# Mixers and experts on one core: first chunk as whole float32, POOL's work elsewhere, router sums moved

## The chip, the core and the metric

The kernel runs on one core of one Trainium2 chip. The metric is device time in microseconds (us). Before the change the median of three runs is 862.81 us (861.21 to 863.67). The engines are PE (TensorE, matrix products), ACT (ScalarE), DVE (VectorE), POOL (GpSimd) and SP, which here only sends for data. Each works its own instructions in order.

## The reference

Two layers, 256 tokens, 1024 channels, everything in float32. A layer is a mixing sublayer and a mixture of experts, each followed by a layer norm over the sum with the residual:

```python
z = h @ w_in[l]                       # ten blocks of 256 columns, and four gates of 1024
branches = (short_conv, rg_lru, gmlp, retention)      # 256 columns each
merged = sum(sigmoid(gate[b]) * (branches[b] @ branch_proj[l, b]) for b in range(4))
h = layer_norm(ALPHA * h + merged @ w_out[l])
# router: one of 4 groups, then 2 of its 8 experts for each token
out = sum(combine[:, e] * ((silu(h @ w_gate[e]) * (h @ w_up[e])) @ w_down[e]) for e in range(32))
h = layer_norm(ALPHA * h + out)
```

## The kernel before

**Weights.** They come in chunks of 1 MB, in the order in which they are used: 34 of a mixing sublayer, then 96 of the experts, then the next layer. `Ring` holds 22 slots of 1 MB; `pump` (line 99) sends for the next chunk on SP's queue whenever a slot beyond the reserve for larger buffers is free, and a few loads of parameters are hung before certain chunks (`before`, line 176): `params` of layer 1 (line 259), with the pack `rp` that holds the router's weights, goes out before the fifth chunk of layer 1.

**The mixing sublayer** (`mixer`, line 350). Every chunk is four pieces of 512 columns. For accuracy a piece is split in two (`do_split`, line 337; `hilo`, line 254): ACT casts it to float32r, which gives the leading bits (`whi`), and DVE subtracts that from the piece (`wlo`). The rows of the layer's input are split in the same way (`hThi`, `hTlo`). A product is then three products (`tripled`, line 323):

```python
nc.tensor.matmul(out, ah, bh, start=first and i == 0, stop=False, skip_group_check=True)
nc.tensor.matmul(out, ah, bl, start=False, stop=False, skip_group_check=True)
nc.tensor.matmul(out, al, bh, start=False, stop=stop_last and i == n - 1, skip_group_check=True)
```

Splits run four pieces (LOOK) ahead of their products. The order of everything else is set by generators: after the products of each piece `advance` (line 463) runs each generator to its next `yield`, so a `yield` is one piece of the sublayer's products. The four branches are such generators: `g_ret` (555), `g_lru` (639), `g_sgu` (683), `g_sc` (721). Some of their elementwise steps are POOL's: the sum of the two rope parts (573), the products of lines 663 and 673, the subtraction of the means in `std64` where it works in place (537), the products 620, 621, 697 and 714, and the Newton steps of the root (`rsqrt`, 305). The retention branch ends in transposes on PE (628), which need line 621.

With the first gate two more things start: `residual` (917), POOL's, which multiplies the rows by ALPHA (layer 0: one instruction of 128x2048; layer 1: also gain and bias of the norm before, from a slot `gb` that SP loads), and `g_router` (280), which sums the router's weights with the norm's gain and bias on PE, DVE and POOL.

**Norm and router** (`norm_mix`, line 780). The rows are summed, their statistics taken, the router's products made from the transposed sums (`rt`, one bank for both halves of the tokens; DVE copies one half, ACT the other), and the logits `lg` formed by four small DVE instructions after the product `raw`.

**The experts** (`moe`, line 1029). For each of eight groups of four experts the tokens are gathered by a product with a one-hot matrix (`gather`, 1142), multiplied with eight chunks (line 1052), and with four more on the way back (1102, 1089). Every chunk gives its slot back when its product is written.

**From layer 0 to layer 1** (`norm_ffn`, line 864). The sums are normalised, turned by PE in 16 transposes, and for each of eight blocks of channels DVE forms the whole rows (`full`, 894), ACT the leading bits (`hThi`, 888), DVE or POOL the rest (`hTlo`, 898), while POOL and ACT split the first pieces of weights. Each pair of neighbouring blocks lies in two PSUM banks.

## Time and profile before

| | us |
|---|---|
| median of three runs | 862.81 |
| lowest, highest | 861.21, 863.67 |
| span of the profiled execution, first to last instruction | 860.7 |
| PE busy | 791.3 (92%) |
| DVE busy | 386.0 (45%) |
| ACT busy | 317.3 (37%) |
| POOL busy | 124.8 (14%) |

Of the profiled execution itself the span is what is recorded. Its mean granted clock of PE is 0.970 of full speed. The shares are means over stages with different limits, so they say little by themselves; the stretches and the waits in them say more. A record of a matrix product is shown with its latency, so consecutive records overlap; how fast they follow each other is read from their starts or from their number in a stretch.

### The profile page before, as it was taken

What the parts mean: (1) busy time and instruction counts of PE and PEld (TensorE: products, weight loads), DVE (VectorE), ACT (ScalarE), POOL (GpSimd) and SP (SyncE); (2) the same over time, 40 slices, a digit from 0 to 9 for tenths busy, and PEclk for the clock granted to TensorE, in tenths of its full rate; (3) what the DMA queues carried; (4) which work ended last, traced back from release to release, by engine and by line L of the source; (5) the groups of instructions that cost most, each with busy time, mean ns of one, the idle gap of its engine ahead of it and who ended that gap; (6) DMA issues with size and microseconds to landing.
All of it is one profiled execution on the core that took longest, in us unless ns stands there. A gap on an engine that the chain in (4) does not pass through costs nothing.

```text
span 860.7 us, 15923 instructions
## 1 busy us (share of the span) xinstructions
PE 791.3 (92%) x6438; PEld 604.1 (70%) x6438; DVE 386.0 (45%) x732; ACT 317.3 (37%) x636; POOL 124.8 (14%) x153
## 2 busy tenths in 40 slices
PE   8999999999999999867889998999999999979794
PEld 7998999999656555422389988999995565544342
DVE  5778677466621111110386779665674211111004
ACT  6564444444523211110356633544444131112012
POOL 4526211011000000000131437110010000000001
PEclk9999999999999999988999999999999999997898
DMA  9986735557799999999997474555587999999994
GB/s 346 425 354 264 253 122 179 191 196 280 323 424 426 426 426 425 425 421 425 424 425 303 158 281 164 183 196 191 175 334 320 426 426 426 425 426 427 423 425 175
DMA packets 40823, 281.07 MB, mean 327 GB/s; under 512 B 4588, under 2 KB 4588, under 8 KB 7456
## 3 DMA queue, kind: packets, MB, share of 16 engines
q1 hardware_dynamic: 40320, 279.20, 80.9%
q8 instruction: 54, 0.88, 0.4%
q10 hardware_dynamic: 288, 0.52, 0.2%
q0 software_dynamic: 128, 0.19, 0.1%
q14 instruction: 33, 0.27, 0.1%
HBM read 278.85 MB, written 1.05 MB: 325 GB/s over the span
## 4 chain that ended last, share of the span: by engine, by line
PE 58%; DMA 27%; DVE 7%; ACT 2%; POOL 1%; issue 1%; SPq 0%; DVEq 0%; ACTq 0%; POOLq 0%
DMA w<-in_exps_dram 25%; PE z L328 9%; PE z L330 9%; PE z L329 9%; PE gu L1052 6%; PE xg L1151 3%; PE y L1102 3%; PE acc L1089 3%; DVE wlo L257 2%; PE pj L330 2%; PE pj L328 2%; PE pj L329 2%; PE acc L328 2%; PE acc L329 2%; PE acc L330 2%; DMA par<-in_par_dram 2%
## 5 line engine op out<-in xcount | busy, mean ns | idle before, releaser
L257 DVE TENSOR_TENSOR wlo<-w,whi 128x512 fp32r<-128x512 f32 x269 | 215.7, 825 | 115.7 <-ACT whi L256 71.6
L330 PE MATMUL z<-hThi,wlo 128*128 128x256 f32 x672 | 192.2, 286 | 3.2 <-DVE wlo L257 3.0
L328 PE MATMUL z<-hThi,whi 128*128 128x256 f32 x672 | 192.5, 286 | 0.4 <-ACT whi L256 0.4
L329 PE MATMUL z<-hTlo,whi 128*128 128x256 f32 x672 | 191.3, 285 | 0.0
L256 ACT CAST whi<-w 128x512 fp32r<-128x512 f32 x272 | 151.4, 618 | 13.4 <-PE z L329 6.7
L1052 PE MATMUL gu<-w,xg 128*32 128x512 f32 x1024 | 128.0, 635 | 22.2 <-PEq L1175 13.0
L330 PEld LDWEIGHTS z<-hThi,wlo 128*128 128x128 f32 x672 | 130.1, 194 | 4.9 <-DVE wlo L257 4.9
L328 PEld LDWEIGHTS z<-hThi,whi 128*128 128x128 f32 x672 | 130.3, 194 | 1.2 <-ACT whi L256 0.7
L329 PEld LDWEIGHTS z<-hTlo,whi 128*128 128x128 f32 x672 | 130.2, 194 | 0.2
L1052 PEld LDWEIGHTS gu<-w,xg 128*32 128x32 f32 x1024 | 30.4, 114 | 98.2 <-issue 65.3
L1157 ACT ACTIVATE xg<-xg,cst 128x128 f32<-128x128 f32 x64 | 25.8, 454 | 167.2 <-PE xg L1151 163.9
L1159 DVE TENSOR_SCALAR xg<-xg,cst 128x128 f32<-128x128 f32 x64 | 23.3, 405 | 129.7 <-PE xg L1151 129.7
L1102 PE MATMUL y<-w,hidT 128*32 128x256 f32 x1024 | 65.4, 383 | 12.8 <-ACT hidT L1082 10.8
L1151 PEld LDWEIGHTS xg<-oh,h 128*128 128x128 f32 x512 | 59.6, 191 | 24.4 <-issue 22.7
L1089 PE MATMUL acc<-y,ct 128*128 128x256 f32 x256 | 68.1, 398 | 1.0 <-ACT y L1106 1.0
L1151 PE MATMUL xg<-oh,h 128*128 128x128 f32 x512 | 65.4, 281 | 0.0
L1089 PEld LDWEIGHTS acc<-y,ct 128*128 128x128 f32 x256 | 44.7, 189 | 25.0 <-issue 11.9
L1102 PEld LDWEIGHTS y<-w,hidT 128*32 128x32 f32 x1024 | 28.9, 109 | 41.1 <-ACT hidT L1082 14.6
L488 POOL TENSOR_TENSOR late<-late 128x512 f32<-128x512 f32 x16 | 25.9, 1616 | 203.9 <-DVE late L483 184.7
L1128 DVE TENSOR_TENSOR ow<-oh,wt 128x256 f32<-128x256 f32 x16 | 6.8, 424 | 106.9 <-PE y L1102 78.8
L1106 ACT COPY y<-y 128x256 f32<-128x256 f32 x64 | 23.8, 373 | 78.6 <-PE y L1102 78.6
L401 ACT ACTIVATE late<-z 128x512 f32<-128x512 f32 x32 | 19.1, 597 | 90.6 <-PE z L330 90.6
(257 smaller groups left out, 1044.4 us busy)
## 6 DMA issues: line engine op xcount, KB each, us to landing
w<-in_exps_dram SPq DMA_DIRECT2D x190, 1024.0 KB, 19.5
w<-in_mixw_dram SPq DMA_DIRECT2D x66, 1024.0 KB, 8.0
w<-in_mixw_dram SPq DMA_DIRECT2D x8, 256.0 KB, 6.2
par<-in_par_dram SPq DMA_DIRECT2D x2, 1024.0 KB, 15.9
w<-in_exps_dram SPq DMA_DIRECT2D x4, 512.0 KB, 17.7
xT<-in_xT_dram SPq DMA_DIRECT2D x4, 256.0 KB, 5.4
h<-in_xtok_dram SPq DMA_DIRECT2D x1, 1024.0 KB, 18.2
gb<-in_fgb_dram SPq DMA_DIRECT2D x1, 1024.0 KB, 5.8
```

Source lines behind the costliest of these rows:

```text
L256: self.nc.scalar.copy(hi, src)
L257: (eng or self.nc.vector).tensor_sub(lo, src, hi.bitcast(F32))
L328: nc.tensor.matmul(out, ah, bh, start=first and i == 0, stop=False, skip_group_check=True)
L329: nc.tensor.matmul(out, ah, bl, start=False, stop=False, skip_group_check=True)
L330: nc.tensor.matmul(out, al, bh, start=False, stop=stop_last and i == n - 1, skip_group_check=True)
L488: nc.gpsimd.tensor_add(a, a, pr)
L1052: nc.tensor.matmul(bank[32 * c:32 * c + 32], xg[g][k // 4][:, k % 4, 32 * c:32 * c + 32], w[:, c], start=k == 0, stop=k == 7, skip_group_c ...
L1089: nc.tensor.matmul(self.W[t][half][:, c0:c0 + 256], ct[:, t * P:t * P + P], y, start=g == 0 and c0 == 0, stop=g == 7, skip_group_check=True)
L1102: nc.tensor.matmul(bank[32 * c:32 * c + 32], hidT[:, f * P + 32 * c:f * P + 32 * c + 32], w[:, f, c], start=f == 0, stop=f == 1, skip_grou ...
L1106: nc.scalar.copy(ys[q], bank)
L1151: nc.tensor.matmul(bank[:, i * P:i * P + P], self.h[:, t, k * P:k * P + P], oh[:, t].rearrange("p e s -> p (e s)"), start=t == 0, stop=t == 1)
L1157: nc.scalar.activation(x[:, 2 * j + i], bank[:, i * P:i * P + P], AF.Identity, bias=b, scale=g)
```

## The change

- The first chunk of each mixing sublayer is no longer split: its 16 products are made of whole float32 operands (`whole_products`). In layer 0 the rows are `xT` as loaded, in layer 1 `full`.
- In `norm_ffn` the blocks are turned in two halves, the second behind the first piece's products. Two neighbouring blocks share a bank, DVE's `full` goes ahead of ACT's `hThi`, all of `hTlo` comes last on DVE, and the four idle products behind the transposes (KW3) are gone.
- POOL's work in the branches (but for the Newton steps and one selection) goes to DVE, with fewer `yield`s behind it; the order of the two products in retention is exchanged.
- The residual becomes a generator of small instructions: on ACT in layer 0, on ACT and DVE in layer 1.
- The router's sums of layer 1 are made behind group 6 of layer 0's experts, and the pack `rp` is loaded before chunk 56 of these experts.
- In `norm_mix` the two halves of `rt` have a bank each and ACT copies both; two of the four small DVE steps go ahead of `raw`, and the negated mean is formed on POOL.
- In `moe` the second half of the first gather moves behind the first two chunks' products.

```diff
+            before[(l - 1) * NCH + NMIX + 56] = [(self.router_params, l)]
...
-        self.splits, self.nsplit = {}, 0
+        self.splits, self.nsplit = {}, 4
...
+                    if u < 4:
+                        self.whole_products(bank, s)
+                        self.do_split(u + LOOK)
+                        u += 1
+                        if s == 3:
+                            del self.ring.tiles[self.base]
+                            self.ring.give(2 if l == 0 else 1)
+                            self.z[n] = bank
+                            self.side(l, n)
+                        self.advance()
+                        continue
...
-                            self.residual(l)
-                            self.gens.append(self.g_router(l))
+                            self.mgens.append(self.g_residual(l))
+                            if l == 0:
+                                self.gens.append(self.g_router(l))
...
+    def whole_products(self, bank, s):
+        w = self.ring.tiles[self.base][:, 512 * s:512 * s + 512].rearrange("p (k c) -> p k c", k=2)
+        x = self.full[s]
+        for kk in range(2):
+            for t in range(2):
+                self.nc.tensor.matmul(bank[:, t * 256:t * 256 + 256], x[:, kk, t * P:t * P + P], w[:, kk],
+                                      start=s + kk + t == 0, stop=(s, kk) == (3, 1), skip_group_check=True)
+        if self.turn_rest and s == 0:
+            self.turn_rest()
...
-        (nc.gpsimd if d is src else nc.vector).tensor_tensor(v3(d), v3(src), s[:, :, None].to_broadcast([P, 8, 64]),
-                                                             op=OP.subtract)
-        yield
-        if d is src:
-            yield
+        nc.vector.tensor_tensor(v3(d), v3(src), s[:, :, None].to_broadcast([P, 8, 64]), op=OP.subtract)
+        yield
...
-            nc.gpsimd.tensor_add(A, A, B)
+            nc.vector.tensor_add(A, A, B)
...
-        yield
-        nc.gpsimd.tensor_tensor(v3(d), v3(d), rs[:, :, None].to_broadcast([P, 8, 64]), op=OP.mult)
-        nc.gpsimd.tensor_mul(d, d, sl)
-        for _ in range(4):
+        nc.vector.tensor_mul(d, d, sl)
+        yield
+        nc.vector.tensor_tensor(v3(d), v3(d), rs[:, :, None].to_broadcast([P, 8, 64]), op=OP.mult)
+        for _ in range(2):
             yield
...
-        nc.gpsimd.tensor_mul(i, i, xc)
+        nc.vector.tensor_mul(i, i, xc)
...
-        nc.gpsimd.tensor_mul(r, r, i)
-        yield
+        nc.vector.tensor_mul(r, r, i)
...
-        nc.gpsimd.tensor_tensor(v3(vg), v3(vg), rs[:, :, None].to_broadcast([P, 8, 64]), op=OP.mult)
-        for _ in range(3):
+        nc.vector.tensor_tensor(v3(vg), v3(vg), rs[:, :, None].to_broadcast([P, 8, 64]), op=OP.mult)
+        for _ in range(2):
...
-        nc.gpsimd.tensor_mul(o, o, ug)
-        yield
+        nc.vector.tensor_mul(o, o, ug)
...
-        rb = self.bank("B", "rt")
+        rbt = [self.bank("W", "rt")[:, :P] for _ in range(2)]
...
-        lt = self.tt("lt", [P, T])
-        nc.vector.tensor_copy(lt[:, :P], rb[:, :P])
-        nc.scalar.copy(lt[:, P:], rb[:, P:256])
+        lt = [self.tt("lt", [P, P]) for _ in range(2)]
+        for t in range(2):
+            nc.scalar.copy(lt[t], rbt[t])
...
         for t in range(2):
-            nc.vector.scalar_tensor_tensor(lm[:, t], self.rbs[:, 0], self.mv[:, t, 0:1], raw[:, t],
+            nc.vector.tensor_scalar(lm[:, t], self.rbs[:, 0], self.mv[:, t, 0:1], None, op0=OP.mult)
+        self.recip(1)
+        for t in range(2):
+            nc.vector.scalar_tensor_tensor(lm[:, t], lm[:, t], self.rs[:, t:t + 1], self.rbs[:, 1],
                                            op0=OP.mult, op1=OP.add)
-        for t in range(2):
-            nc.vector.scalar_tensor_tensor(lg[:, t], lm[:, t], self.rs[:, t:t + 1], self.rbs[:, 1],
+            nc.gpsimd.tensor_scalar(self.nm[:, t:t + 1], self.mv[:, t, 0:1], -1.0, None, op0=OP.mult)
+            nc.gpsimd.tensor_mul(self.nm[:, t:t + 1], self.nm[:, t:t + 1], self.rs[:, t:t + 1])
+        for t in range(2):
+            nc.vector.scalar_tensor_tensor(lg[:, t], raw[:, t], self.rs[:, t:t + 1], lm[:, t],
                                            op0=OP.mult, op1=OP.add)
...
-            if half == 0:
-                self.do_split(0, nc.gpsimd)
-        self.do_split(1, nc.gpsimd)
...
-        self.keep_warm(KW3, "B")
...
+        banks = [self.bank(tag, "htp") for tag in "PPWW"]
+        self.full = [self.tt("full").rearrange("p (i t) -> p i t", i=2) for _ in range(4)]
+        block = lambda k: banks[k // 2][:, k % 2 * 256:k % 2 * 256 + 256]
+
+        def turn(q):
+            for k in range(4 * q, 4 * q + 4):
+                for t in range(2):
+                    nc.tensor.transpose(block(k)[:, t * P:t * P + P], h[:, t, k * P:k * P + P], self.ident)
+            for k in range(4 * q, 4 * q + 4):
+                nc.vector.tensor_scalar(self.full[k // 2][:, k % 2], block(k), self.col(l, "fg", k),
+                                        self.col(l, "fb", k), op0=OP.mult, op1=OP.add)
+                nc.scalar.activation(self.hThi[:, k], block(k), AF.Identity, bias=self.col(l, "fb", k),
+                                     scale=self.col(l, "fg", k))
+            if q:
+                for i in range(4):
+                    c = slice(2 * i, 2 * i + 2)
+                    nc.vector.tensor_sub(self.hTlo[:, c], self.full[i], self.hThi[:, c].bitcast(F32))
+
+        turn(0)
+        self.turn_rest = lambda: turn(1)
+
+    def g_residual(self, l):
+
         nc = self.nc
         self.needs[self.layer] -= 1
+        rows = self.h.rearrange("p t c -> p (t c)")
         if l == 0:
-            nc.gpsimd.tensor_scalar(self.h, self.h, ALPHA, None, op0=OP.mult)
+            for i in range(4):
+                yield
+                nc.scalar.mul(rows[:, 512 * i:512 * i + 512], rows[:, 512 * i:512 * i + 512], ALPHA)
             return
...
+        for _ in range(14):
+            yield
+        for i in range(4):
+            nc.scalar.mul(gb[:, 512 * i:512 * i + 512], gb[:, 512 * i:512 * i + 512], ALPHA)
+            yield
+        for i in range(4):
+            c = slice(512 * (i % 2), 512 * (i % 2) + 512)
+            x = rows[:, 512 * i:512 * i + 512]
+            nc.vector.tensor_mul(x, x, gb[:, c])
+            yield
+            yield
+            nc.vector.tensor_add(x, x, gb[:, 1024 + c.start:1024 + c.stop])
+            yield
+            yield
+        self.ring.give()
...
-        next(first[1])
...
-                if (g, k) == (0, 3):
+                if g == 0 and k < 2:
                     next(first[1], None)
...
+            if g == 6 and l + 1 < L:
+                for _ in self.g_router(l + 1, "B"):
+                    pass
```

## Rows read from the trace of the kernel before

**Rows 1.** Busy time of engines by stretch; columns: PE, PEld, DVE, ACT, POOL, PEclk, DMA share, GB/s.

```profile
56.00:74.00 18.00, 15.62 (x127) 15.01 (x126) 16.97 (x29) 9.75 (x18) 12.89 (x21) 1.00 0.74 288
97.00:107.00 10.00, 10.00 (x86) 10.00 (x85) 5.21 (x8) 4.05 (x8) 0.00 (x0) 1.00 0.61 202
430.00:437.00 7.00, 5.79 (x40) 4.72 (x38) 6.69 (x12) 3.65 (x9) 2.67 (x3) 1.00 1.01 423
```

**Rows 2.** The same view, start and length of the experts' transfers in both layers.

```profile
231.00:234.00 3.00, 3.00 (x29) 2.42 (x32) 1.37 (x4) 1.46 (x3) 0.00 (x0) 1.00 0.06 19
234.00:423.00 189.00, 165.65 (x1447) 86.25 (x1443) 25.43 (x74) 38.69 (x100) 0.00 (x0) 0.95 1.00 421
661.00:846.00 185.00, 166.37 (x1439) 87.40 (x1431) 24.03 (x69) 40.19 (x103) 0.64 (x1) 0.94 1.00 420
```

**Rows 3.** Waits of the whole span: who waited for whom, us in total, times, longest.

```profile
PE rtp L628 <- POOL ret L621: 4.2, 2, 2.1
...
ACT lt L825 <- DVE lt L824: 1.4, 2, 0.7
```

**Rows 4.** Waits from 440 to 540 us, in layer 1's mixing sublayer.

```profile
PE z L330 <- DVE wlo L257: 2.4, 3, 1.1
```

**Rows 5.** Busy time by stretch, right behind the wait at line 628 in layer 0.

```profile
74.00:76.00 2.00, 2.00 (x15) 2.00 (x14) 0.99 (x3) 0.00 (x0) 1.49 (x7) 0.72 0.75 303
76.00:78.00 2.00, 2.00 (x11) 2.00 (x11) 1.34 (x2) 0.00 (x0) 1.23 (x2) 0.50 0.00 0
```

**Rows 6.** The chain that ended last: start us, us, what.

```profile
35.63 0.87 PE lu L658 x4
...
230.41 2.91 PE xg L1151 x24
...
511.40 1.02 PE rb L286 x16
516.92 0.56 PE rb L296 x4
...
529.35 2.87 DVE wlo L257
```

**Rows 7.** Timeline of the first pieces: start us, us, instruction, idle before it and releaser.

```profile
5.16 0.62 ACT L256 CAST whi<-w 128x512 fp32r<-128x512 f32 x1 [0.79 <-DMA w<-in_mixw_dram]
...
5.83 0.58 PE L328 MATMUL z<-whi,hThi 128*128 128x256 f32 x1 [1.13 <-ACT whi L256]
```

**Rows 8.** Groups of instructions: count, busy us, mean ns, idle before them and releasers.

```profile
L257 DVE TENSOR_TENSOR wlo<-w,whi 128x512 fp32r<-128x512 f32 x269 | 215.7, 825 | 115.7 <-ACT whi L256 71.6 <-PE z L330 30.8 <-PE z L329 8.2
...
L888 ACT ACTIVATE hThi<-htp,cst 128x256 fp32r<-128x256 f32 x8 | 4.2, 567 | 3.4 <-DVE full L894 3.4
...
L894 DVE TENSOR_SCALAR full<-htp,cst 128x256 f32<-128x256 f32 x8 | 4.0, 534 | 0.6 <-ACT hThi L888 0.6
...
L318 POOL TENSOR_TENSOR ryr<-ryr,rzr 128x8 f32<-128x8 f32 x6 | 3.2, 542 | 0.5
...
L553 DVE TENSOR_TENSOR ret<-z,ret 128x512 f32<-128x512 f32 x2 | 1.4, 679 | 0.0
```

**Rows 9.** Timeline of POOL ahead of the transposes of line 628, layer 0.

```profile
70.57 1.49 POOL L620 TENSOR_TENSOR ret<-ret,ryr 128x512 f32<-128x512 f32 x1
72.13 1.59 POOL L621 TENSOR_TENSOR ret<-ret 128x512 f32<-128x512 f32 x1
```

**Rows 10.** DMA issues: engine, count, KB each, median us to landing.

```profile
rp<-in_rp_dram SPq DMA_DIRECT2D x2, 384.5 KB, 15.3
```

**Rows 11.** Timeline of DVE at the router's logits, layer 0.

```profile
226.32 0.42 DVE L835 SCALAR_TENSOR_TENSOR lm<-rbs,mv,lg 128x40 f32<-128x40 f32 x2 [0.86 <-PE lg L828]
```

**Rows 12.** Timeline of DVE at the turn into layer 1.

```profile
428.59 0.54 DVE L894 TENSOR_SCALAR full<-htp,cst 128x256 f32<-128x256 f32 x1
429.73 0.54 DVE L894 TENSOR_SCALAR full<-htp,cst 128x256 f32<-128x256 f32 x1 [0.60 <-ACT hThi L888]
```

**Rows 13.** Timeline of PE: first product of layer 1's second chunk.

```profile
440.10 0.28 PE L328 MATMUL z<-whi,hThi 128*128 128x256 f32 x1
```

More of the change, by code (lines that the diff above doesn't have):

```diff
@@ L257, in hilo, with router_params @@
         (eng or self.nc.vector).tensor_sub(lo, src, hi.bitcast(F32))
+    def router_params(self, l):
+        rp = self.lp.tile([P, 769], F32, name="rp")
+        self.nc.sync.dma_start(rp, self.a["rp"][l])
+        self.bsb = rp[:, :256].rearrange("p (c t) -> p c t", c=2)
+        self.wr = rp[:, 256:768].rearrange("p (k e) -> p k e", k=8)
+        self.rb = rp[:, 768:]
     def params(self, l):
-        nc, a, lp = self.nc, self.a, self.lp
+        nc, a = self.nc, self.a
         par = self.ring.take("par")
@@ L278, in done_with_params, with g_router @@
             self.ring.give()
-    def g_router(self, l):
+    def g_router(self, l, tag="W"):
         nc = self.nc
         gb = self.col(l, "mg", 0, 16).rearrange("p (i k) -> p i k", i=2)
-        bank = self.bank("W", "rb")
+        bank = self.bank(tag, "rb")
         for k in range(8):
@@ L293, in g_router @@
         yield
-        bank = self.bank("W", "rb")
+        bank = self.bank(tag, "rb")
         for i in range(2):
@@ L403, in mixer @@
                         if (j, bp) == (0, 0):
-                            self.residual(l)
-                            self.gens.append(self.g_router(l))
-                        if (j, bp) == (4, 0) and l:
-                            ring.give()
+                            self.mgens.append(self.g_residual(l))
+                            if l == 0:
+                                self.gens.append(self.g_router(l))
                         if (j, bp) == (7, 1):
@@ L797, in logits @@
                 o = i % 2 * 64
-                nc.tensor.matmul(rb[o:o + 64, t * P:t * P + P], self.wr[:, 4 * q + i], xT[t, q][:, i],
-                                 start=t + q == 0 and i < 2, stop=q == 1 and i > 1, skip_group_check=True)
+                nc.tensor.matmul(rbt[t][o:o + 64, :], self.wr[:, 4 * q + i], xT[t, q][:, i],
+                                 start=q == 0 and i < 2, stop=q == 1 and i > 1, skip_group_check=True)
         for t in range(2):
@@ L874, in norm_ffn @@
                 self.normalise(t, half, self.W[t][half], t == half)
-            if half == 0:
-                self.do_split(0, nc.gpsimd)
-        self.do_split(1, nc.gpsimd)
-        blocks = {}
-        banks = [self.bank(tag, "htp") for tag in "PPWWWW"]
-        for k, b in enumerate((0, 1, 2, 4, 3, 5, 3, 5)):
-            blocks[k] = banks[b][:, k // 6 * 256:k // 6 * 256 + 256]
-            for t in range(2):
-                nc.tensor.transpose(blocks[k][:, t * P:t * P + P], h[:, t, k * P:k * P + P], self.ident)
@@ L884, in norm_ffn @@
-        self.keep_warm(KW3, "B")
-        full = {}
-        def high(k):
-            nc.scalar.activation(self.hThi[:, k], blocks[k], AF.Identity, bias=self.col(l, "fb", k),
-                                 scale=self.col(l, "fg", k))
-        def whole(k):
-            if k % 2:
-                full[k // 2] = self.tt("full").rearrange("p (i t) -> p i t", i=2)
-            nc.vector.tensor_scalar(full[k // 2][:, k % 2], blocks[k], self.col(l, "fg", k), self.col(l, "fb", k),
-                                    op0=OP.mult, op1=OP.add)
@@ L897, in low @@
-        def low(k, eng):
-            eng.tensor_sub(self.hTlo[:, k], full[k // 2][:, k % 2], self.hThi[:, k].bitcast(F32))
-        V, G = nc.vector, nc.gpsimd
-        for a in (0, 2, 4, 6):
-            high(a)
-            whole(a + 1)
-            high(a + 1)
-            whole(a)
-            if a < 4:
-                low(a, V)
-                low(a + 1, V)
-            else:
-                low(a, G)
-                low(a + 1, V)
-            if a == 0:
-                self.do_split(2, G)
@@ L914, in norm_ffn @@
-        for u in range(3, LOOK):
-            self.do_split(u)
-    def residual(self, l):
+        banks = [self.bank(tag, "htp") for tag in "PPWW"]
[14 more added lines that the diff above has]
+                    nc.vector.tensor_sub(self.hTlo[:, c], self.full[i], self.hThi[:, c].bitcast(F32))
@@ L926, in residual @@
         nc.sync.dma_start(gb, bass.AP(tensor=src.tensor, offset=src.offset + (l - 1) * 2048, ap=[[0, P], [1, 2048]]))
-        nc.gpsimd.tensor_scalar(gb, gb, ALPHA, None, op0=OP.mult)
-        for t in range(2):
-            nc.gpsimd.tensor_mul(self.h[:, t], self.h[:, t], gb[:, :1024])
-            nc.gpsimd.tensor_add(self.h[:, t], self.h[:, t], gb[:, 1024:])
+        for _ in range(14):
[13 more added lines that the diff above has]
+        self.ring.give()
     def route(self, l):
@@ L1243, in build @@
         k.hilo(flat(k.hThi[:, c]), flat(k.hTlo[:, c]), flat(k.xT[:, c]))
-        if i < LOOK:
-            k.do_split(i)
-    for u in range(4, LOOK):
-        k.do_split(u)
+    k.full, k.turn_rest = [k.xT[:, 2 * i:2 * i + 2] for i in range(4)], None
     k.gens = [rope]
-    k.ring.give()
     for l in range(L):
```

15 lines of the change are left out of this document (6 added, 9 removed).

## The prediction

> **What bounds the kernel now.** I read the busy time of the engines by stretch first, then the waits of the tensor engine (PE), then the timelines at the places where it waits. Each layer is a mixing sublayer followed by experts, and the two halves have different limits. In a quiet stretch of the mixing sublayer PE is busy all the time: 86 products in 10 us, so one product of split operands passes every 0.116 us [rows 1]. Earlier in the same sublayer, where the four branches are worked, PE is busy for 15.62 of 18 us and DVE for 16.97 [rows 1]: there DVE is as full as PE, and PE waits. The experts are bound by the weights' DMA. It is nearly idle from 231 to 234 us (share 0.06) because the ring is full, and from 234 to 423 it runs at 1.00 and 421 GB/s; the second layer does the same from 661 to 846 [rows 2]. The restart comes when the first expert product has freed the first slot. So what is saved ahead of that product counts in full, what is saved behind it counts for nothing, and bytes added to that stretch count in full.
>
> In the list of waits, PE's two longest in the mixing sublayers are both for POOL's product with the silu gate, at the transposes of line 628: 4.2 us in 2 times [rows 3]. Waits for the lower part of split weights (wlo, line 257) make 2.4 us in the branch part of the second sublayer [rows 4]. [...]
>
> **The change, part by part.** The profiled execution spans 860.7 us; the median of the runs is 862.8, so 2.1 us lie around the span. I let them stand and count differences.
>
> (a) *First chunk of layer 0.* 48 split products at 0.116 us are 5.6 us. A whole float32 product of this shape is two records: line 658 has two products in the source and four records in 0.87 us [rows 6], 0.217 each. So 16 x 2 x 0.217 = 6.9 us: dearer on PE by 1.3 us at full clock. Against that the first product no longer waits for the cast that starts at 5.16 us and releases it at 5.83 [rows 7], and eight instructions of ACT and DVE fall away. The end of the chunk is tied to transfers that do not move. I take 0, between -0.7 (those 5.83 - 5.16 us) and +1.3.
>
> (b) *POOL's work to DVE and ACT.* Nine instructions per sublayer go to DVE: two rope sums, the subtraction of the means in the gMLP branch, and two products each in the recurrence, the retention and the gMLP branch. On DVE a 128x512 product takes 679 ns [rows 8], so 6.1 us are added per sublayer; on POOL the last two of retention took 1.49 and 1.59 us [rows 9]. DVE also gets something back: its splits average 825 ns [rows 8], and beside POOL's work one of them takes 2.87 us [rows 6]. DVE has room: in the quiet stretch it is busy 5.21 of 10 us [rows 1]; in the full one four of the nine land (2.7 us), against about as much relief. If that cover is missing, the added time shows at PE (the slower rival).
>
> At line 628 two things change. The two products shrink from 3.1 to 1.4 us, and the transposes, written six yields behind the end of the root, are now four behind it, so PE comes there two pieces (2 x 12 x 0.116 = 2.8 us) earlier. Moreover POOL no longer does the gMLP subtraction in between, so its Newton steps end earlier; but DVE must now wait for them with splits queued behind it. I take the wait of 2.1 us down to 0.9, and the clock's 1.6 us to 0.5 (it may or may not still fall): 2.3 us per layer, 4.6 in all, between 0 and 2 x 3.7 = 7.4. The other waits for DVE: most of the 2.4, say 2.2, since layer 1's residual (where POOL held DVE for 2.87 us) is now small instructions of ACT and DVE spread over 34 pieces; less 0.2 per layer for new waits. I take 1.8, between 2.4 and a loss of 8.2 (below). Layer 0's residual is four instructions on ACT, busy 4.05 of 10 us there: nothing. The residual's load of gb is sent at the same place; its slot comes free ten pieces earlier.
>
> (c) *Router sums among the experts, layer 1.* Out of the PE-bound sublayer go 1.02 and 0.56 us of PE [rows 6]: -1.6. They come back behind group 6, where PE waits for weights anyway: nothing. Their parameters, 384.5 KB [rows 10], move ahead of 40 expert chunks into the DMA-bound stretch: 0.394 MB / 421 GB/s = +0.9 us. In SP's queue that load waits for readers that ended in the norm long before, so it holds no chunk; at its old place it cost nothing.
>
> (d) *End of the mixing sublayer.* Two of the four small DVE steps behind the router's product (0.42 us as a pair [rows 11], 0.34 to the next) move ahead of it. The copies of the sums get a bank each; before, ACT waited 0.7 us for DVE's copy each time [rows 3]. I take 0.65 per layer, between 0.3 and 1.0: -1.3 in all. The four tiny steps on POOL end before ACT is free for the rows.
>
> (e) *First gather.* Of 24 records in 2.91 us [rows 6] the last 8 move behind the first expert product, so the first slot comes free 0.95 us earlier: -1.9 in all, nothing to -1.9. The second half is needed only from the fifth chunk on.
>
> (f) *Turn into layer 1.* In 430 to 437 us PE starts 40 products where 60 would fit, and DVE is busy 6.69 of 7 us [rows 1]: the first chunk there takes some 9.7 us for 5.6 us of work, because it waits for the split rows. Now it needs only the whole rows, but the next chunk needs all that was put off. The order matters: two blocks now share a bank, and DVE and ACT both read each block. At 429.73 DVE had waited 0.60 us for ACT on the same block [rows 12], and ACT waited for DVE on the other half of one bank at line 825 [rows 3]. So I count an alternation: per pair of blocks DVE, ACT, DVE, 534 + 567 + 534 ns [rows 8] or 1.63 us, four pairs 6.5, then four subtractions and the first wlo at about 0.68, 3.4: 9.9 us from 428.6, where DVE has normalised the rows and turns to the first block [rows 12], to 438.5, or 439 with the handovers. Then 11 of 12 products remain of the next chunk's first piece, 1.3 us. It began at 440.10 before [rows 13], and so ended at 441.5; now it ends near 440.3: -1.2, between -2.6 and +4.4. [...] Were only a block's own bytes ordered, DVE's 8 x 0.534 + 5 x 0.68 would end by 436.3, PE's own 6.9 us and its transposes would bind, and the term would be -2.6.
>
> Sum: 0 - 4.6 - 1.8 - 1.6 + 0.9 - 1.3 - 1.9 - 1.2 = -11.5; 862.8 - 11.5 = **851.3 us**.
>
> **The rivals.** *Wait and lower clock gone*: DVE reaches the retention products after the roots are ready, as POOL's shorter queue suggests; then -7.4 in place of -4.6, and with (f) at -2.4 it is 847.3. *The wait stays* at line 628 because DVE comes late: 4.6 less, 855.9; for it, DVE is the fullest engine just there. [...]
>
> *Slower: DVE becomes the bound* between 56 and 84 us and in the same stretch of layer 1. If POOL's relief does not come, because its 24 tiny Newton steps (542 ns on average in the retention branch [rows 8]) remain and DVE now waits in order for them, then six moved instructions x 0.68 = 4.1 us per layer pass straight to PE, and nothing of (b) is gained: 862.8 - 1.6 + 0.9 - 1.3 - 1.9 - 1.2 + 8.2 = 865.9. The point that decides is the lead of four pieces, 5.6 us, that the splits have over PE: only delay beyond it is seen. [...] At half that price it is 861.8, no change.
>
> **How the numbers follow.** Forecast 0.48, wait gone 0.16, wait stays 0.12, clock at the turn 0.08, DVE at half price 0.08, at full price 0.08. About 0.3% (2.6 us) is what measurement can tell from no change: faster 0.84, same 0.08, slower 0.08. The range 845 to 860 takes in the first four and the bounds of (a), (d), (e) and (f), and leaves out the two DVE cases and a little below.
>
> **What would show it.** Right: no wait over 1 us at the transposes of line 628's successor and a clock of 1.00 behind it; wlo near 0.7 us without splits of 2 us and more; the DMA restarting about 5 us earlier in layer 0; second-sublayer PE without the sums of line 286; the stretch of DMA at 1.00 longer by 0.9 us in layer 0 alone. Wrong: new waits for wlo in the branch stretch, DVE idle behind POOL's Newton steps, or a granted clock under 1.00 in the first chunk of layer 1.

## The result and the profile after

The median is **853.37 us** (851.45 to 853.73, four runs) against 862.83 of the kernel before (861.21 to 863.67, four runs): ratio 0.9888, 95% interval 0.9873 to 0.9902. The gain of 9.5 us is in the range forecast (851.3; 845 to 860), 2 us short of the 11.5 that its sum gave. The profiled execution spans 851.8 us, 8.9 less than before.

What the starts of single products in the two traces say, in us:

| first of its kind | before | after | gained so far |
|---|---|---|---|
| q's turned rows, layer 0 (rtp) | 26.45 | 25.89 | 0.6 |
| router's product (rt) | 223.09 | 219.20 | 3.9 |
| gather (xg) | 230.40 | 225.80 | 4.6 |
| expert product (gu) | 233.25 | 227.75 | 5.5 |
| last sum of layer 0's experts (acc) | 425.21 | 420.56 | 4.7 |
| recurrence's product, layer 1 (lu) | 459.68 | 453.80 | 5.9 |
| router's product (rt) | 649.60 | 636.71 | 12.9 |
| gather (xg) | 656.91 | 643.30 | 13.6 |
| expert product (gu) | 659.76 | 645.25 | 14.5 |
| last sum of layer 1's experts (acc) | 850.47 | 841.44 | 9.0 |

So 14.5 us were won on the way into layer 1's experts, and **5.5 us of them were lost again inside these experts**. The waits of layer 1's mixing sublayer after the change (who waited for whom, us in total, times, longest):

```profile
PE z L334 <- DVE wlo L258: 1.2, 1, 1.2
PE rtp L651 <- DVE ret L644: 1.0, 1, 1.0
PE z L335 <- DVE wlo L258: 0.6, 2, 0.3
```

The wait at the retention transposes is 1.0 where it was 2.1 [rows 3]; the waits for wlo were 2.4 by one line alone [rows 4]. The stretches of the profile after, in which the first two answer [rows 5] and the others [rows 1, 2] (us; busy time of PE, PEld, DVE, ACT, POOL; granted clock, DMA share, GB/s):

```profile
70.00:72.00 2.00, 2.00 (x19) 2.00 (x18) 0.50 (x2) 0.00 (x0) 1.45 (x6) 1.00 0.75 315
72.00:74.00 2.00, 2.00 (x25) 1.70 (x24) 2.00 (x5) 0.00 (x0) 0.00 (x0) 1.00 0.00 0
...
52.00:70.00 18.00, 16.70 (x136) 16.09 (x135) 15.84 (x32) 9.63 (x18) 7.59 (x19) 1.00 0.86 336
424.00:431.00 7.00, 6.75 (x36) 5.52 (x35) 4.43 (x10) 3.95 (x8) 0.31 (x1) 1.00 1.00 422
...
646.00:834.00 188.00, 167.76 (x1415) 87.09 (x1415) 23.94 (x69) 39.26 (x100) 0.64 (x1) 0.93 0.99 414
834.00:842.00 8.00, 7.33 (x72) 4.10 (x64) 3.06 (x8) 2.97 (x6) 0.00 (x0) 1.00 0.00 0
```

Behind the transposes the clock stays at 1.00. DVE, with POOL's work added, is busy for less of the branch stretch, 15.84 us and not 16.97. Its splits are shorter: in these two stretches they last 685 ns on average after 857, and the whole group of 264 takes 731 ns after 825 [rows 8]:

```profile
L258 DVE TENSOR_TENSOR wlo<-w,whi 128x512 fp32r<-128x512 f32 x264 | 187.6, 731 | 112.5 <-ACT whi L257 71.0 <-PE z L335 27.6 <-PE z L334 7.2
```

The last two stretches show what was not foreseen. Before, the last transfer set the end: the last weights landed at 847.6 and the last sum ended 3.2 us behind them. Now the weights have landed by 834.1 and PE works on until 841.8, 7.8 us longer. The timeline of PE (records of weight loads left out), before and then after, at the branch behind group 5 (`overflow`, line 1198, code for experts with too many tokens, which here is jumped over):

```profile
800.80 1.99 PE L1089 MATMUL acc<-y,ct 128*128 128x256 f32 x8
808.35 7.22 PE L1052 MATMUL gu<-w,xg 128*32 128x512 f32 x48 [5.55 <-PEq L1175]
...
788.09 1.99 PE L1109 MATMUL acc<-y,ct 128*128 128x256 f32 x8
795.84 1.93 PE L1072 MATMUL gu<-w,xg 128*32 128x512 f32 x7 [5.76 <-DMA w<-in_exps_dram]
801.01 7.81 PE L1072 MATMUL gu<-w,xg 128*32 128x512 f32 x41 [3.24 <-issue]
...
808.75 2.05 PE L1174 MATMUL xg<-oh,h 128*128 128x128 f32 x16
```

PEq is PE's sequencer. Seven products behind the branch PE now stands still for 3.24 us with nothing to wait for that the profile shows ("issue"), and from 793 to 807 its granted clock is 0.51. In the kernel before the 48 products ran through: the way from the last product ahead of the branch to the end of these 48 took 12.8 us there and 18.7 here.

The trace also has PE's own instructions arriving by DMA, in blocks of 16 KB (54 on that queue in the span). From 37.2 to 363.9 us, over 21 blocks, PE left 2641 records of products and 2639 of weight loads, 251 a block, and in the kernel before 2642 and 2641 over 21 blocks (37.6 to 366.9), 252. With the instructions that leave no such record (branches, semaphores) I take a block as 256, an estimate that the places of the stalls bear out. One block came at 793.0 and the next at 798.8. In layer 1 of all 14 profiled runs the block that follows the first one behind this branch came 5.4 to 5.8 us after it, 2.7 to 3.0 us after PE had begun to work again. PE stood still for 5.76 us at this branch; what it waited for there no run shows. Counted in the built programs, the change moves the place behind layer 1's branch by 180 instructions within its block of 256, from 193 ahead of a block's end to 13 ahead of one. Seven products are 14 instructions (a weight load and a product each), so PE stands still where the block ends, to within one instruction.

### The profile page after: what moved, and what is told of

It reads as the page before. It is cut to its first block, busy times and chain, and to the rows that moved or that the text cites. A ratio compares the mean times of both kernels' runs of the same rounds, so it can differ in the third digit from the quotient of the medians.

```text
span 851.8 us, 15820 instructions
## 1 busy us (share of the span) xinstructions
PE 787.8 (92%) x6402; PEld 598.9 (70%) x6402; DVE 369.2 (43%) x749; ACT 317.4 (37%) x638; POOL 72.1 (8%) x132
## 4 chain that ended last, share of the span: by engine, by line
PE 34%; DMA 16%; DVE 4%; ACT 2%; issue 1%; DVEq 0%; SPq 0%; ACTq 0%
DMA w<-in_exps_dram 16%; PE z L335 5%; PE z L333 5%; PE z L334 5%; PE gu L1072 5%; PE y L1122 2%; PE acc L1109 2%; PE xg L1174 2%; PE pj L335 1%; PE pj L334 1%; PE pj L333 1%; PE acc L333 1%; PE acc L335 1%; PE acc L334 1%; DVE wlo L258 1%
## 5 line engine op out<-in xcount | busy, mean ns | idle before, releaser
L258 DVE TENSOR_TENSOR wlo<-w,whi 128x512 fp32r<-128x512 f32 x264 | 187.6, 731 | 112.5 <-ACT whi L257 71.0
L1072 PE MATMUL gu<-w,xg 128*32 128x512 f32 x1024 | 129.9, 639 | 24.1 <-DMA w<-in_exps_dram 14.9
L257 ACT CAST whi<-w 128x512 fp32r<-128x512 f32 x264 | 146.9, 617 | 12.6 <-PE z L335 5.3
L1109 PEld LDWEIGHTS acc<-y,ct 128*128 128x128 f32 x256 | 44.7, 189 | 25.0 <-issue 11.5
```

The costliest lines, as they stand in the source:

```text
L257: self.nc.scalar.copy(hi, src)
L258: (eng or self.nc.vector).tensor_sub(lo, src, hi.bitcast(F32))
L1072: nc.tensor.matmul(bank[32 * c:32 * c + 32], xg[g][k // 4][:, k % 4, 32 * c:32 * c + 32], w[:, c], start=k == 0, stop=k == 7, skip_group_c ...
L1109: nc.tensor.matmul(self.W[t][half][:, c0:c0 + 256], ct[:, t * P:t * P + P], y, start=g == 0 and c0 == 0, stop=g == 7, skip_group_check=True)
```

## The experiments

Each ran with the kernel before on the same chip; intervals are 95%. Not all ran on one chip, so experiments are compared by their ratios to the kernel before. "The mark" is the shifted kernel of the first experiment. Where the code that PE runs was changed, the place behind the branch was kept away from a block's end.

**1. Move the block's end (shift).** In layer 1's groups 1 to 4:

```diff
+            if l and 1 <= g <= 4:
+                bank = self.bank("B", "pad")
+                for _ in range(3):      # 12, 13 in the next two
+                    nc.tensor.matmul(bank[:, :40], self.ident, self.cst[:, C_SEL:C_SEL + 40], ...)
```

> The changed kernel with 12 small float32 products (128x40, read by nothing) in the second layer's expert groups 1 to 4, where PE has slack: they move the place behind the branch at line 1198 in PE's instruction stream from 13 instructions ahead of the end of a block of 256 to 24 behind the start of one (counted in the built program). Theory A, the block's end: in the profile PE runs 7 products behind the branch and then stands still for 3.2 us while the next 16 KB of its instructions arrive, and its clock stays at half until 806.9. With 230 instructions left in the block the stall goes, the time from the last product ahead of the branch to the end of the 48 products behind it falls from 18.7 us to some 12.8 (as before the change), the experts end with the weights' transfers again, and the time falls from 853.4 by some 4.6 to about 848.8 us. Theory B, PE is late at the end of the second layer because the transfers restart earlier in relation to the branch: the stall moves or stays, and the time is within 1 us of 853.4. Theory C, the products added cost more than the stall: above 854.

Measured 849.27 us (848.55 to 849.73), ratio 0.9863 (0.9846 to 0.9881). PE's timeline behind the branch:

```profile
789.70 1.99 PE L1109 MATMUL acc<-y,ct 128*128 128x256 f32 x8
797.43 7.40 PE L1072 MATMUL gu<-w,xg 128*32 128x512 f32 x48 [5.74 <-PEq L1203]
```

The stall is gone, the last sum comes at 837.45 instead of 841.44. By the ratios the gain is smaller, so the changed kernel was run again beside other experiments.

> The changed kernel once more, unaltered, beside the runs of this call: 0.989 of the kernel before (0.9873 to 0.9902). If the gain of 2.5 us that the shifted products gave is real, it stays 2 to 4 us above that kernel's 0.9863.

It gave 851.89 us, 0.9879 (0.9863 to 0.9894), with a stall of 3.1 us at the same place. The stall is in both profiled executions of the changed kernel. By the ratios it costs 1.4 us (0.9879 less 0.9863) to 2.2 (0.9888), and there the intervals overlap. By the traces, from layer 1's first expert product to its last sum, it costs 2.2 to 4.0 us (194.4 and 196.2, against 192.2 in the mark).

**2. Make the stall in the kernel before.** The same lines with 12 products a group.

> The kernel before with 48 such products in the second layer's groups 1 to 4, so that the place behind the branch comes to 12 instructions ahead of the end of a block (it is 193 ahead now). Theory A: PE now stands still for about 3 us some 7 products behind the branch in the second layer, its clock stays at half for some 7 us longer, and the time grows from 862.8 by 2 to 4.6 us (PE comes to the branch 1.8 us earlier in relation to the transfers here than in the changed kernel, so that some of it is caught up). Theories B and C: no stall behind the first products; 862.8 within 1 us, or a little more for the products added, with no gap behind the branch.

Measured 871.82 us, 1.0126 (1.0108 to 1.0144). The stall came to the product where it was counted to be, but the price was more than twice what was expected: 48 products more are not free.

```profile
816.27 1.93 PE L1052 MATMUL gu<-w,xg 128*32 128x512 f32 x6 [5.69 <-PEq L1180]
821.41 8.17 PE L1052 MATMUL gu<-w,xg 128*32 128x512 f32 x42 [3.21 <-issue]
```

So the same with 13 a group:

> The kernel before with 52 small products in the second layer's groups 1 to 4, four more than in the run with 48: the place behind the branch moves 16 instructions on, from 12 ahead of a block's end to 4 behind the start of the next one. The run with 48 took 1.0126 of the kernel before (10.9 us), which is more than the stall and the lower clock can account for (3.2 + 3.4 us), so the products added have a price too. Theory A: the stall is gone although there are more products, the half clock behind the branch is 6.8 us long and not 13.7, and the time is 4 to 6.5 us below the run with 48, at 1.005 to 1.008 of the kernel before. Theory C, the products alone made that run slow: 1.013 or more, with no fall.

Measured 869.32 us, 1.0073 (1.0059 to 1.0087): more products, less time, by 0.53% or 4.6 us, and no stall.

```profile
817.88 6.81 PE L1052 MATMUL gu<-w,xg 128*32 128x512 f32 x48 [5.68 <-PEq L1180]
```

The stall by the block's end is shown in both directions. Its price is clear of the noise in the kernel before alone; in the changed kernel its place and its absence are clear, its price is not.

**3. Give PE slack instead.** Layer 1 has another long wait: at 755.7 PE waits 4.1 us for four rows that POOL's queue has just sent for, then works at a granted clock of 0.50 until 772.7. The rows are sent for two groups earlier, the stall stays:

```diff
+            if g == 2 and l + 1 == L:
+                self.rows = self.wr.rearrange("p k e -> p (k e)")
+                nc.gpsimd.dma_start(self.rows[0:4], ...)
...
-        rows = self.tt("rows")
-        nc.gpsimd.dma_start(rows[0:4], ...)
+        rows = self.rows
```

> The changed kernel with one move: the 4 rows of the last norm's gain and bias are sent for at the end of the second layer's group 2 instead of group 4, into the router's weights, which are done with. PE's order and the 13 instructions ahead of the block's end stay as they are, so the stall of 3.2 us behind the branch is expected again. Theory A, sharpened: the stall costs something only because PE has no slack left in the second layer: at 755.7 it waits 4.1 us for these rows and works at half clock until 772.7. Without this wait PE comes to the branch some 6 to 9 us earlier in relation to the transfers, catches up behind the stall, and the end is again set by the last transfer: 849 us, as with the shifted products. Theory B, the end is set by the stall itself: 853.4, no change. Were PE alone the limit, the whole 7 us or more would be gained: below 847.

Measured 849.91 us, 0.9856 (0.9841 to 0.9871), 2.0 us better than the changed kernel beside it (the intervals overlap a little). Its waits in layer 1's experts:

```profile
PE gu L1072 <- PEq L1201: 5.8, 1, 5.8
...
PE gu L1072 <- issue: 3.3, 1, 3.3
PE gu L1072 <- DMA w<-in_exps_dram: 1.7, 2, 1.4
```

The stall is as long as before, and costs nothing that shows (0.9856, the mark 0.9863): PE waits for transfers again, and the last sum ends 2.8 us behind the last weights (7.8 and 6.0 in the changed kernel, 3.9 in the mark). Layer 1's experts were thus not simply bound by DMA, as the prediction took from their share of 1.00; PE's long stops together had used up its slack.

**4. The retention products back on POOL.** From here on one part of the change is undone in the shifted kernel.

```diff
-        nc.vector.tensor_mul(d, d, sl)
         yield
-        nc.vector.tensor_tensor(v3(d), v3(d), rs[...], op=OP.mult)
-        for _ in range(2):
+        nc.gpsimd.tensor_tensor(v3(d), v3(d), rs[...], op=OP.mult)
+        nc.gpsimd.tensor_mul(d, d, sl)
+        for _ in range(4):
```

> The changed kernel, shifted as in the run with 12 small products (whose 0.9863 of the kernel before, 849.3 us, is the mark here), with one part undone: the two products behind the root of the retention branch (lines 642 and 644) are POOL's again, in the old order and with the old count of yields ahead of the transposes. The forecast put 2.3 us per layer on this place: 4.6 us slower (853.9), with waits of about 2 us at the transposes of line 651's successor in both layers and a granted clock of 0.5 behind them. Rival: the place is only where PE happened to wait, and the gain came from the other seven instructions moved and from the residual: within 1.5 us of 849.3, with the wait's time turning up elsewhere. Second rival: it is worth the bound of 3.7 us per layer: 856.7.

Measured 854.64 us, 0.9895 (0.9878 to 0.9912): 2.8 us by the ratios, 4.7 in the trace at layer 1's first expert product, 1.6 from layer 0 and 2.9 from layer 1's mixing sublayer. The forecast's 4.6 for this place agrees with the trace; by the ratios it is less, with intervals that overlap. The clock, expected to fall in both layers, fell in layer 1 alone (0.59 and 0.56 behind the transposes), which is most of what the two layers differ by. The wait itself comes out as two (layer 0):

```profile
PE rtp L651 <- POOL ret L644: 1.4, 1, 1.4
PE sv L727 <- DVE sgu L719: 1.1, 1, 1.1
```

**5. The other seven back on POOL** (`nc.vector` to `nc.gpsimd` at lines 563, 596, 686, 696, 719 and 736, with the old yields; line 563 serves gMLP).

> The changed kernel with the shift of 12 small products (mark: 0.9863 of the kernel before, 849.3 us), and the other seven of the nine branch instructions back on POOL with their old yields (rope sums, the subtraction of means and three products of recurrence and gMLP); the two retention products stay on DVE. Putting those two back cost 1.6 us in the first layer and 2.9 in the second by the starts of the first expert products, which leaves some 1.7 and 2.5 us of part (b) for these seven and the residual. Theory A, these seven carried what the forecast undersized: the first expert product comes 1.5 us later in the first layer and 1.5 to 2.5 in the second, 3 to 4 us in all (852 to 853.5). Theory B, the residual carried it: nothing in the first layer, under 1 us in the second (849 to 850.5). Theory C, DVE is better off without them: faster than 849.

Measured 851.67 us, 0.9881 (0.9864 to 0.9899): 1.6 us. In the trace 2.0 in layer 0, where the wait at the transposes is 2.1 again and the clock falls behind it, and 0.2 in layer 1, where the wait is 2.1 too and the clock stays up. By the time it is less than theory A and more than B, and the intervals overlap that of the mark.

**6. The residual back on POOL** (`g_residual` to `residual` of the kernel before).

> The same shifted kernel with the residual back on POOL, all at once (two instructions of 128x2048 and four of 128x1024). Theory A of the run beside it (the seven): under 1 us in either layer. Theory B: the first layer unchanged, the second 2 to 2.5 us later, because splits of 2 us and more come back beside POOL's long instructions and PE waits for wlo: 851.3 to 852. The forecast had 1.8 us for it, less 0.2 per layer.

Measured 856.89 us, 0.9937 (0.9922 to 0.9952): 6.4 us, more than any theory said. The first expert product comes 2.05 us later in layer 0 and 6.7 in layer 1; 5.1 of these arise in layer 1's own mixing sublayer (the recurrence's product there is 1.6 late). Layer 0's part is rather 2.8: in this execution q's turned rows came 0.74 earlier than in the mark, ahead of anything that differs. The clock stayed at 1.00 in both mixing sublayers here, so it has no part in these numbers. The timelines of POOL and DVE, layer 0 and layer 1:

```profile
71.34 5.87 POOL L931 TENSOR_SCALAR h<-h 128x2048 f32<-128x2048 f32 x1
...
71.90 4.13 DVE L258 TENSOR_TENSOR wlo<-w,whi 128x512 fp32r<-128x512 f32 x1
...
512.85 2.79 POOL L938 TENSOR_TENSOR h<-h,gb 128x1024 f32<-128x1024 f32 x1
515.72 2.73 POOL L939 TENSOR_TENSOR h<-h,gb 128x1024 f32<-128x1024 f32 x1
...
514.25 10.96 DVE L258 TENSOR_TENSOR wlo<-w,whi 128x512 fp32r<-128x512 f32 x5 [0.88 <-ACT whi L257]
```

A split that takes 0.67 us alone takes 4.13 beside POOL's instruction of 5.87, and of the five beside the shorter ones, which take 2.71 to 2.85, three take 2.87 to 2.89. PE's waits for wlo in layer 1 are then

```profile
PE z L335 <- DVE wlo L258: 4.7, 5, 1.9
```

where the mark has 0.6, and from 505 to 525 PE is busy for 15.73 us, where it is busy for all 20 in the mark.

**7. The residual alone.** Is that only so because DVE now has nine instructions more? The kernel before with `g_residual` and nothing else:

> The kernel before with one part of the change alone: the residual on ACT and DVE, spread over pieces, in both layers; nothing else moves, and the place behind the branch stays 193 instructions ahead of a block's end. Putting the residual back on POOL in the shifted changed kernel cost 2.05 us in the first layer and 5.1 in the second by the starts of the first expert products. Theory A, the residual on POOL costs so much only where DVE also has the nine moved instructions: here the move gives no more than the forecast's 1.8 us, all in the second layer: 861 us. Theory B, it costs the same beside any load of DVE: 2 us in the first layer and 5 in the second, 855 to 857. Theory C, DVE's four products and sums cost more here than POOL's: slower.

Measured 858.07 us, 0.9943 (0.9927 to 0.9960): 4.9 us; in the trace 1.7 in layer 0 and 3.1 in layer 1's mixing sublayer. Between A and B. By the ratios the residual on POOL costs about 5 us by itself, and some 1.5 more where DVE is fuller, which is within the noise of the two. The traces say more, once the clock is made equal. In layer 0 the clock fell behind the wait at line 628 in the kernel before and not here, and that is 0.8 of the 1.7. In the first run of experiment 2, whose code up to there is that of the kernel before, it did not fall either (it has 1.00 where [rows 5] has 0.72 and 0.50):

```profile
74.00:76.00 2.00, 1.68 (x14) 1.68 (x15) 1.53 (x4) 0.00 (x0) 1.59 (x7) 1.00 0.93 385
76.00:78.00 2.00, 1.85 (x16) 1.65 (x14) 1.48 (x4) 0.00 (x0) 1.75 (x4) 1.00 0.05 20
```

From q's transposes to the experts of layer 0 that run takes 205.99 us, the kernel before 206.80 and this one 205.25. So the residual alone is worth 0.7 us in layer 0 and 3.1 in layer 1, and beside DVE's nine moved instructions 2.8 and 5.1.

**8. The first chunk of layer 1 split again**, with the old turn of `norm_ffn`.

> The same shifted kernel with the turn into the second layer and its first chunk as before: products of split operands, the eight blocks in six banks, splits on POOL. The forecast gave this part 1.2 us, by an alternation of DVE and ACT on shared banks, and the traces of the two kernels have the recurrence's first products 1.2 us closer: 850.5. Theory B, the whole products are worth more, since the other changes left DVE fuller at the turn: 852 or more. Theory C, worth nothing by the end of the layer: 849.3.

Measured 852.81 us, 0.9885 (0.9866 to 0.9904): 1.9 us. In the trace, from layer 0's last sum to the recurrence's products, it takes 36.5 us, against 33.2 in the mark and 34.5 in the kernel before. With the rest of the change in place the old turn is worse than it was, and the clock falls behind it:

```profile
431.00:436.00 5.00, 3.15 (x22) 2.55 (x22) 4.64 (x7) 4.01 (x8) 2.24 (x3) 1.00 1.00 423
436.00:440.00 4.00, 4.00 (x24) 4.00 (x23) 2.66 (x5) 1.29 (x3) 0.00 (x0) 0.57 1.01 428
```

**9. The order at the turn.** After the change DVE reads the eight blocks like this (ACT the same, between):

```profile
424.01 0.54 DVE L912 TENSOR_SCALAR full<-htp,cst 128x256 f32<-128x256 f32 x1
425.19 0.99 DVE L912 TENSOR_SCALAR full<-htp,cst 128x256 f32<-128x256 f32 x2 [0.63 <-ACT hThi L914]
426.82 1.12 DVE L912 TENSOR_SCALAR full<-htp,cst 128x256 f32<-128x256 f32 x2 [0.64 <-ACT hThi L914]
428.57 1.00 DVE L912 TENSOR_SCALAR full<-htp,cst 128x256 f32<-128x256 f32 x2 [0.63 <-ACT hThi L914]
430.20 0.54 DVE L912 TENSOR_SCALAR full<-htp,cst 128x256 f32<-128x256 f32 x1 [0.64 <-ACT hThi L914]
```

```diff
-                nc.scalar.activation(self.hThi[:, k], block(k), ...)
+                a = k ^ 2
+                nc.scalar.activation(self.hThi[:, a], block(a), ...)
```

> The same shifted kernel, with ACT taking the blocks of each half of the turn in the order 2, 3, 0, 1 while DVE takes 0, 1, 2, 3, so that the two never want the same bank at once; the instructions and the banks are the same. Theory A, the alternation on shared banks bounds the turn (in the changed kernel DVE waits 0.63 us for ACT and ACT 0.61 for DVE at every pair, eight blocks take from 424.01 to 430.7): each half now takes about 2.2 us instead of 3.3, the split products of the second chunk start up to 1.6 us earlier (PE's own whole products end near 432), and the time falls by 1 to 1.6 us, to 848. Theory B, the order is fixed by something else than the bank: no change, 849.3. Theory C, ACT's late blocks hold up the lower parts: slower by up to 1.

Measured 848.51 us, 0.9835 (0.9819 to 0.9851), 2.4 us better than the mark by the ratios (the intervals overlap). From layer 0's last sum to the recurrence's products it takes 1.2 us less (32.06 instead of 33.24), in the 1 to 1.6 that theory A asked for. DVE's eight blocks take 5.5 us instead of 6.7, and not the 4.4 of theory A, for about 0.5 us of waiting is left at every pair:

```profile
424.87 0.99 DVE L912 TENSOR_SCALAR full<-htp,cst 128x256 f32<-128x256 f32 x2
426.36 0.99 DVE L912 TENSOR_SCALAR full<-htp,cst 128x256 f32<-128x256 f32 x2 [0.50 <-ACT hThi L915]
427.93 0.99 DVE L912 TENSOR_SCALAR full<-htp,cst 128x256 f32<-128x256 f32 x2 [0.58 <-PE htp L910]
429.42 1.00 DVE L912 TENSOR_SCALAR full<-htp,cst 128x256 f32<-128x256 f32 x2 [0.49 <-ACT hThi L915]
```

**10. The three moves that helped, together.**

> The changed kernel with all three moves that helped: 12 small products for the shift, the order 2, 3, 0, 1 of ACT at the turn, and the rows of the last norm sent for at group 2. The run with the first two took 0.9835 of the kernel before. Theory A, with the stall gone the end is set by the last transfers again, and the rows' 3.4 to 4.1 us of waiting and the half clock behind it lie in slack: at most 0.6 us more, 0.983 (848 us). Theory B, PE was still the limit there: 3 us or more, below 0.980 (845 us).

Measured **848.07 us** (847.43 to 848.56), 0.9826 (0.9807 to 0.9844), the lowest time and ratio of all, as theory A had it, though within the interval of experiment 9. PE waits for transfers in layer 1's experts five times, 5.7 us in all.

## Why the prediction was right, and where it was not

The time was forecast within 2.1 us, but by terms that missed in both directions.

- **(a)** 0 forecast; 0.6 gained at q's transposes, where executions of the same code differ by 1.5 among themselves (25.21 in the second run of the changed kernel, 26.69 in experiment 3). Nothing that can be measured.
- **(b), the place of the wait**: 4.6 forecast, 4.5 by the undoing of the two products in the trace (1.6 and 2.9). The wait fell to 1.0 (0.9 forecast). The lower clock was oversized, though: the sum has 1.6 us a layer for it, taken down to 0.5, and no run shows a loss of 1.6. The code of layer 0 and of layer 1's mixing sublayer is the same in the kernel before and in experiment 2. In its first run the clock stayed up in both layers; from q's transposes to layer 0's experts it took 0.8 us less, and 0.9 less from the recurrence to the experts of layer 1. In its second run the clock fell in both, and these times are those of the kernel before to 0.1 us. So a fall costs 0.8 to 0.9 us here, not 1.6, and it does not come in every execution.
- **(b), the residual: the step that failed.** "Layer 0's residual is four instructions on ACT ...: nothing", and for the other waits 1.8 in all. I priced the instructions that come and not the one that goes: POOL's single instruction of 5.75 us in layer 0 had held one of DVE's splits for 4.12. In the kernel before, and PE's wait for splits in layer 0 there:

```profile
84.54 5.75 POOL L922 TENSOR_SCALAR h<-h 128x2048 f32<-128x2048 f32 x1
84.97 4.12 DVE L257 TENSOR_TENSOR wlo<-w,whi 128x512 fp32r<-128x512 f32 x1
...
PE z L330 <- DVE wlo L257: 0.7, 2, 0.4
```

  Alone the move is worth 0.7 and 3.1 us with the clock made equal, 3.8 where 1.8 was forecast; taken back out of the whole change it is worth 2.8 and 5.1. All of (b) came to 8.7 us where 6.4 was forecast: 3.3 in layer 0 (3.9 less (a)) and 5.4 in layer 1 (12.9 less the 5.9 of the recurrence and the 1.6 of (c)). Its parts don't add up: undone singly they cost 6.6 in layer 0, counted from q's transposes (1.5, 2.3, 2.8), and 8.2 in layer 1 (2.9, 0.2, 5.1).
- **What POOL's work does to DVE's was weighed in one direction.** The rows of experiment 6 show DVE's subtractions of two SBUF operands held beside POOL's long instructions. Beside POOL's products of 2.71 to 2.85 us three of five subtractions last as long (2.87 to 2.89, and 0.67 alone), but beside the instruction of 5.75 us one is held for 4.12, and the two subtractions behind it (89.02 and 89.62) take 0.68 each while POOL's record still runs, to 90.29. What holds them no run shows. I weighed DVE's waiting for POOL, in the rivals in which POOL's relief does not come; the larger effect was the relief when POOL's long instructions went. Those rivals, DVE as the bound, did not come.
- **(c)** 1.6 of PE's work went out of layer 1's sublayer as said; it was not undone by itself, so its worth there is taken from [rows 6] and not measured. From layer 0's first expert product to its last sum it takes 192.8 us instead of 192.0: 0.85 against the 0.9 forecast for `rp`, but (e) is in it too.
- **(d)** 1.3 forecast; from the router's product to the gather 0.7 us are gained per layer, 1.4 in all.
- **(e)** The first expert product comes 0.9 us earlier in each layer, as said, but whether the transfers keep that is open. The second and third slot come free only after two more pieces of the gather, so in both layers the first three chunks are sent for 2.1 us apart, and not 0.9. The eighth chunk lands 25.6 us after the first expert product in both layers; in the trace before it was 24.5, but 24.9 to 25.7 in experiments 2 and 7, which have the old order. The stretches behind the restart in layer 0, two before and three after, where 421 GB/s would be the full rate [rows 2]:

```profile
236.00:238.00 2.00, 2.00 (x24) 1.06 (x16) 0.00 (x0) 0.45 (x3) 0.00 (x0) 1.00 0.86 365
238.00:240.00 2.00, 2.00 (x18) 0.56 (x19) 0.00 (x0) 0.81 (x2) 0.00 (x0) 1.00 1.05 438
...
230.00:232.00 2.00, 2.00 (x20) 1.05 (x16) 0.68 (x2) 1.81 (x5) 0.00 (x0) 1.00 0.75 258
232.00:234.00 2.00, 2.00 (x20) 0.59 (x24) 0.00 (x0) 0.81 (x2) 0.00 (x0) 1.00 1.11 385
234.00:236.00 2.00, 2.00 (x20) 0.77 (x13) 0.00 (x0) 0.00 (x0) 0.00 (x0) 1.00 0.93 311
```

  That what is saved ahead of the first expert product counts in full, as the prediction has it, holds only if the slots behind it come as fast as the transfers. (e) was not undone by itself, and the traces don't settle it: layer 1's experts take 192.2 us in the mark and 190.7 before, but 191.8 in experiment 7, without (e).
- **(f)** 1.2 forecast, 1.2 measured (34.5 to 33.2 us), and by the mechanism named: DVE and ACT alternate on the shared banks, eight blocks in 424.01 to 430.7, 6.7 us against 6.5. Experiment 9 bears it out: with the two on other banks at the same time the eight blocks take 5.5. The order of the program keeps the two apart on a bank, so this says nothing on what the chip would do without it. No run shows the 4.4 us of the upper bound, a lower clock at the turn: after the change the granted clock was 1.00 from 424 to 440.
- **Not foreseen**: the stall behind the branch, 1.4 to 4.0 us, and that PE had no slack to make up for it. "The experts are bound by the weights' DMA" did not hold for the end of layer 1.

The sum came close by luck: (b), with its undersized residual, brought 2.3 us more than forecast, and the stall took 1.4 to 4.0 that were not in the sum, with what may be missing of (e).

## What to carry to other kernels

When work leaves POOL, price first what its long instructions did to DVE's: look for DVE records of several times their usual length beside them (4.12 us where others took 0.68). Where a kernel branches, count where the place behind the branch falls in its block of instructions; the change moved it by 180 instructions, onto a stall of 3.24 us, and 12 small products ahead of it took the stall away. And a stretch with a DMA share of 1.00 is bound by DMA only as long as PE catches up with its longest stops: compare when the last transfer lands and when the work behind it ends (3.2 us apart before the change, 7.8 after it).

## What the runs showed of the hardware

- At the branch over `overflow`, which also reads the value that decides it, PE stood still for 5.5 to 7.4 us in both layers of every profiled run. With 12 or 13 instructions left in the block that it lands in, it stood still for another 3.1 to 3.3 us, since the next block came 5.5 to 5.7 us after the first (793.0 and 798.8 in the changed kernel). In layer 1 no run has a place between 13 and 193. PE went on 5.0 to 5.3 us after it had begun, and the kernels without the stall begin 32 to 36 products in that time, so by an estimate places with up to some 60 instructions left would stall too, for less.
- One instruction of POOL of 5.87 us held a subtraction on DVE for 4.13 us, and not to its end; beside POOL's shorter products of 2.71 to 2.85 us three of five subtractions took 2.87 to 2.89, about as long as these, and so did the one of 2.87 in [rows 6], beside an instruction of POOL of 2.71.
- The same instructions of the mixing sublayers ran with and without a fall of the clock at the wait of line 628 in different executions, with 0.8 to 0.9 us between them. Over all profiled runs the clock fell behind a wait of 2.1 us in 6 of 10 places, behind one of 1.4 in 1 of 2, and behind one of 1.0 in none of 16.
